# Summing the squares of the RMS norms over the d tiles with vector additions in place of partial matmuls

## The chip, the cores and the metric

The kernel runs on one core of one Trainium2 chip. The time is the device time of one execution in microseconds; where there are several runs, their median is given.

## The reference

Two layers of a trunk over 256 latent tokens and 256 context tokens of width 1024. Each layer normalises, mixes (attention and a recurrent branch), normalises again and applies a SwiGLU channel mixer, dense in layer 0 and top-2 of 8 experts in layer 1. The part that matters here is the norm, which needs the sum of squares of each token over its 1024 channels:

```python
def rms_norm(x, g):
    xf = x.astype(jnp.float32)
    y = xf * lax.rsqrt(jnp.mean(xf * xf, axis=-1, keepdims=True) + EPS)
    return (y * g.astype(jnp.float32)).astype(x.dtype)
...
    for i in range(DEPTH):
...
        a_lat = modulate(rms_norm(h_lat, mix_norm_g[i]), sh1, sc1)
        a_ctx = modulate(rms_norm(h_ctx, mix_norm_g[i]), csh1, csc1)
...
        h_lat = h_lat + g1 * o_lat
...
        h_lat = h_lat + g2 * ffn(modulate(rms_norm(h_lat, ffn_norm_g[i]), sh2, sc2))
```

## The kernel before

The residual stream is kept transposed in SBUF: `hctx` and `hlat` each hold 8 tiles (d = 0 to 7) of 128 channels by 256 tokens. Both streams together are 512 columns, one PSUM bank in f32. Because the channels lie on the partitions, a token's sum of squares goes over 8 tiles and 128 partitions.

Three passes use `stat_add` and `stat_end`. Pass 1 runs at the start, over the loaded input. Pass 2 runs inside the out-projection of layer 0 (`mixer`): when a tile d of the projection is done, `resid` adds it to the residual stream (L611), and `stat_add` squares the new tile, the context half on ScalarE and the latent half on VectorE. Pass 3 does the same in the last of the four down-projections of layer 0's FFN (`ffn`). A later norm, ahead of the experts, and the final one are computed in other functions.

In a pass, tiles 0 to 6 are each multiplied by a 128x32 block of ones (L553). The 32 output rows go to one of four strips of the bank `part`, by d mod 4, so that the bank ends with four partial sums, each 32 times over. With tile 7 ScalarE copies the bank, divided by 32 (L547), and two matmuls with a full block of ones give the sum on all partitions in the bank `ss`: one over the copy (L549), one over tile 7's squares (L550). `stat_end` then takes an inverse square root on ScalarE (`y0`, L560) and refines it with four VectorE steps (L561 to L564); `scaled` and `mod1` apply scale and shift and split the result into `ah` and `al`, with which the next matmuls begin.

Full products are made of three fp32r matmuls, L311, L312 and L313, over a high and a low half of both operands. Weights are loaded into `raw` buffers by SP's queue (L212), ScalarE makes `hi` of them (L276) and VectorE the rest, `lo` (L288); four pairs of `hi` and `lo` are held, and a new one is made when TensorE has done with an old one. An out-projection group has 24 such matmuls, a down-projection group 21.

Other work stands in between: adaLN products over weight chunks (L415 in pass 2 and after pass 3; L480 and L486 at the start, in `ada_first`), their rows' copy and transposes (L419, L422), sums over rows for `g2row` and `rbc` (L457, L459, L1103 to L1108), and warm-up matmuls at the start (L360). Which instruction stands where in an engine's queue is decided when the program is built, by a scheduler with costs of its own. The small PSUM pool "T" has two banks, and `part`, `ss` and the sums above take turns in it.

Of the kernel before, what the change touches and what calls it, by code (L numbers as in the profile page):

```python
# [12 lines left out]
AF = mybir.ActivationFunctionType  # L13
# [6 lines left out]
ND = D // P  # L20
NCTX = 256
NLAT = 256
T = NCTX + NLAT
# [165 lines left out]
class Trunk:  # L189
# [340 lines left out]
    def stat_add(self, d, t0, at):  # L530
        nc = self.nc
        n = T - t0
        if d == 0:
            self.part = self.bank("T")
        sq = self.t2k(nm="sq")
        for s in range(t0 // NCTX, 2):
            o, h = sq[:, s * NCTX - t0:(s + 1) * NCTX - t0], self.h(d, s)
            if s < SQ[at]:
                a = nc.scalar.activation(o, h, AF.Square)
            else:  # L540
                nc.vector.tensor_mul(o, h, h)
        if d == 0:
            with self.tc.issue_after(a.ins):
                self.preload(AF.Abs_reciprocal_sqrt, self.epst[0:1, 0:1])
        if d == ND - 1:
            ps = self.t2k(nm="part")
            nc.scalar.activation(ps[:, :n], self.part[:, :n], AF.Copy, scale=1.0 / 32)  # L547
            self.ss = self.bank("T")
            nc.tensor.matmul(self.ss[:, :n], lhsT=self.ones, rhs=ps[:, :n], start=True, stop=False)  # L549
            nc.tensor.matmul(self.ss[:, :n], lhsT=self.ones, rhs=sq[:, :n], start=False, stop=True)  # L550
            return
        g = 32 * (d % 4)
        nc.tensor.matmul(self.part[g:g + 32, :n], lhsT=self.ones[:, :32], rhs=sq[:, :n], start=d < 4, stop=d >= 3, tile_position=(0, g))  # L553

    def stat_end(self, t0, after=None):
        nc = self.nc
# [1047 lines left out]
```

## Time and profile before

| | |
|---|---|
| median of 3 runs | 1809.37 us (1807.25 to 1811.66) |
| profiled execution, its own time | 1812.09 us |
| its span | 1810.3 us |
| TensorE busy | 1764.0 us, 97% |
| VectorE busy | 1051.0 us, 58% |
| ScalarE busy | 824.7 us, 46% |
| HBM read | 484.94 MB, 268 GB/s over the span |
| mean granted TensorE clock | 0.984 |

Busy shares are means over stages with different limits. A row of the timeline gives an instruction's start, its duration, engine, line and operands; "x2" behind it says that neighbouring instructions were merged, and the brackets give the idle time of the engine ahead of it and what ended that. Matmuls overlap, so the distance between two starts says more than a duration. An f32 matmul appears as two instructions. PE is TensorE's matmuls, PEld its weight loads, DVE VectorE, ACT ScalarE.

### The profile page before, as it was taken

The numbers are of one execution on the slowest core, as the hardware profiler recorded it, in microseconds if no ns is written. First come the engines' busy times: TensorE is split into PE (matmuls) and PEld (weight loads), VectorE is DVE, ScalarE is ACT, GpSimd is POOL, SyncE is SP. The second block draws the span as 40 slices with busy tenths as digits, with TensorE's granted clock in tenths as the row PEclk, the third lists the DMA queues.
The fourth block names the chain that finished last, engine by engine and source line by source line (L and its number), as shares of the span: only waits on it lengthen the run. The fifth ranks groups of instructions, "written<-read, shape, count | busy, mean of one in ns | idle before, by whom it ended". The sixth has DMA issues, their size and how long they took to land. (4 is left out here: it accounts for less than half of the span.)

```text
span 1810.3 us, 22890 instructions
## 1 busy us (share of the span) xinstructions
PE 1764.0 (97%) x8645; PEld 1249.9 (69%) x8645; DVE 1051.0 (58%) x1611; ACT 824.7 (46%) x1200; POOL 0.5 (0%) x5
## 2 busy tenths in 40 slices
PE   8999999999999999999999999999999999999996
PEld 5776766888888888578887437788536883378632
DVE  4785636883555433488758119999406981189611
ACT  3674624222222222277647117777315871178512
POOL 0000000000000000000000000000000000000000
PEclk8999999999999999999999999999999999999998
DMA  9551235452534323243355999999899999999995
GB/s 383 219 206 65 68 145 199 160 199 93 181 141 182 143 89 116 94 153 113 137 221 239 388 421 421 421 421 410 343 422 421 421 420 411 421 421 420 408 416 221
DMA packets 72261, 487.55 MB, mean 269 GB/s; under 512 B 8144, under 2 KB 10576, under 8 KB 15952
## 3 DMA queue, kind: packets, MB, share of 16 engines
q1 hardware_dynamic: 71856, 485.49, 67.2%
q8 instruction: 70, 1.15, 0.2%
q10 hardware_dynamic: 288, 0.52, 0.1%
q14 instruction: 47, 0.39, 0.1%
HBM read 484.94 MB, written 1.05 MB: 268 GB/s over the span
## 5 line engine op out<-in xcount | busy, mean ns | idle before, releaser
L276 ACT ACTIVATE hi<-raw 128x1024 fp32r<-128x1024 f32 (+1 forms) x470 | 478.7, 1051 | 440.8 <-PE ps L312 316.9
L288 DVE TENSOR_TENSOR lo<-raw,hi 128x1024 fp32r<-128x1024 f32 (+1 forms) x470 | 549.1, 1211 | 105.2 <-ACT hi L276 102.9
L311 PE MATMUL ps<-ah,hi 128*128 128x512 f32 (+1 forms) x1024 | 396.6, 393 | 6.7 <-ACT ah L590 6.1
L313 PE MATMUL ps<-ah,lo 128*128 128x512 f32 (+1 forms) x1024 | 394.6, 386 | 0.0
L312 PE MATMUL ps<-al,hi 128*128 128x512 f32 (+1 forms) x1024 | 393.7, 385 | 0.0
L325 PE MATMUL ps<-hi,xe 128*128 128x512 f32 x888 | 241.4, 394 | 7.4 <-ACT hi L276 7.4
L311 PEld LDWEIGHTS ps<-ah,hi 128*128 128x128 f32 x1024 | 192.7, 189 | 61.1 <-issue 16.2
L313 PEld LDWEIGHTS ps<-ah,lo 128*128 128x128 f32 x1024 | 192.9, 188 | 45.3 <-issue 7.1
L312 PEld LDWEIGHTS ps<-al,hi 128*128 128x128 f32 x1024 | 193.4, 189 | 38.3 <-issue 2.1
L1363 PE MATMUL ps<-raw,x 128*64 128x512 f32 x896 | 202.3, 594 | 0.0
L325 PEld LDWEIGHTS ps<-hi,xe 128*128 128x128 f32 x888 | 166.8, 189 | 46.2 <-ACT hi L276 10.5
L1363 PEld LDWEIGHTS ps<-raw,x 128*64 128x64 f32 x896 | 64.5, 137 | 124.2 <-issue 123.0
L327 PE MATMUL ps<-lo,xe 128*128 128x512 f32 x444 | 139.9, 397 | 0.8 <-DVE lo L288 0.8
L1351 DVE TENSOR_TENSOR gts<-gts,ps 128x256 f32<-128x256 f32 x28 | 11.8, 422 | 211.6 <-ACT gts L1350 211.6
L1340 ACT ACTIVATE s<-ps 128x512 f32<-128x512 f32 x28 | 16.7, 597 | 221.7 <-PE ps L1363 221.7
L1386 PE MATMUL ps<-raw,gts 128*64 128x512 f32 x440 | 106.0, 599 | 0.5 <-DMA raw<-in_moe_dn_dram 0.5
L327 PEld LDWEIGHTS ps<-lo,xe 128*128 128x128 f32 x444 | 82.5, 189 | 21.3 <-issue 2.8
L611 DVE SCALAR_TENSOR_TENSOR hctx<-ps,ada,hctx 128x256 f32<-128x256 f32 x40 | 19.3, 484 | 107.8 <-PE ps L313 107.6
L325 PE MATMUL ps<-hi,ah 128*128 128x512 f32 x224 | 71.5, 400 | 0.0
L325 PE MATMUL ps<-hi,al 128*128 128x512 f32 x224 | 69.6, 392 | 0.0
L327 PE MATMUL ps<-lo,ah 128*128 128x512 f32 x224 | 69.1, 390 | 0.0
L335 ACT ACTIVATE ah<-ps 128x512 fp32r<-128x512 f32 x44 | 26.3, 599 | 92.6 <-PE ps L1258 51.5
(279 smaller groups left out, 1757.5 us busy)
## 6 DMA issues: line engine op xcount, KB each, us to landing
raw<-in_moe_up_dram SPq DMA_DIRECT2D x222, 1024.0 KB, 16.4
raw<-in_moe_dn_dram SPq DMA_DIRECT2D x111, 1024.0 KB, 17.3
raw<-in_adaw_dram SPq DMA_DIRECT2D x48, 1024.0 KB, 4.8
raw<-in_ffn_up_dram SPq DMA_DIRECT2D x28, 1024.0 KB, 4.8
raw<-in_w_in_dram SPq DMA_DIRECT2D x20, 1024.0 KB, 6.1
raw<-in_ffn_dn_dram SPq DMA_DIRECT2D x16, 896.0 KB, 4.6
raw<-in_w_out_dram SPq DMA_DIRECT2D x8, 1024.0 KB, 4.9
aux<-in_bias_dram SPq DMA_DIRECT2D x16, 192.0 KB, 3.7
```

What stands on the lines that cost most here:

```text
L276: self.his.append(self.nc.scalar.activation(hi[:, :m], raw[:, i * m:(i + 1) * m], AF.Copy))
L288: self.lastlo = self.nc.vector.tensor_sub(lo[:, :m], raw[:, i * m:(i + 1) * m], hi[:, :m])
L311: mm(out, lhsT=l[0], rhs=r[0], start=start, stop=False)
L312: mm(out, lhsT=l[0], rhs=r[1], start=False, stop=False)
L313: mm(out, lhsT=l[1], rhs=r[0], start=False, stop=stop)
L325: mm(out, lhsT=x[i], rhs=w[0][:, c], start=start and i == 0, stop=False)
L327: mm(out, lhsT=x[0], rhs=w[1][:, c], start=False, stop=stop)
L335: self.nc.scalar.activation(hi, src, AF.Copy)
L611: self.nc.vector.scalar_tensor_tensor(h, src[:, s * NCTX - t0:(s + 1) * NCTX - t0], self.ada[l][:, g, d, s:s + 1], h, ALU.mult, ALU.add)
L1340: nc.scalar.activation(s, h, AF.Copy)
L1363: nc.tensor.matmul(ps[j * SMALL:(j + 1) * SMALL], lhsT=xf[k], rhs=chs[j][:, kk * 512:(kk + 1) * 512], start=k == 0, stop=k == ND - 1, tile ...
L1386: nc.tensor.matmul(py[hf * SMALL:(hf + 1) * SMALL], lhsT=gt[f], rhs=ch[ff * 2 + hf], start=f == 0, stop=f == NF - 1, tile_position=(0, hf ...
```

## The change

The partial matmuls into strips, their bank and its copy go. The squares of tile 0 are kept, and VectorE adds the squares of tiles 1 to 6 to them, one addition per tile. With tile 7 there are two matmuls with the full block of ones, over the running sum and over tile 7's squares, into the same bank `ss`.

```diff
     def stat_add(self, d, t0, at):
         nc = self.nc
         n = T - t0
-        if d == 0:
-            self.part = self.bank("T")
         sq = self.t2k(nm="sq")
...
-        if d == ND - 1:
-            ps = self.t2k(nm="part")
-            nc.scalar.activation(ps[:, :n], self.part[:, :n], AF.Copy, scale=1.0 / 32)
+        if d == 0:
+            self.part = sq
+        elif d < ND - 1:
+            nc.vector.tensor_add(self.part[:, :n], self.part[:, :n], sq[:, :n])
+        else:
             self.ss = self.bank("T")
-            nc.tensor.matmul(self.ss[:, :n], lhsT=self.ones, rhs=ps[:, :n], start=True, stop=False)
-            nc.tensor.matmul(self.ss[:, :n], lhsT=self.ones, rhs=sq[:, :n], start=False, stop=True)
-            return
-        g = 32 * (d % 4)
-        nc.tensor.matmul(self.part[g:g + 32, :n], lhsT=self.ones[:, :32], rhs=sq[:, :n], start=d < 4, stop=d >= 3, tile_position=(0, g))
+            for i, x in enumerate((self.part, sq)):
+                nc.tensor.matmul(self.ss[:, :n], lhsT=self.ones, rhs=x[:, :n], start=i == 0, stop=i == 1)
```

The scheduler also moves instructions around the passes. Lines behind `stat_add` are three lower in the changed kernel (L608 is the old L611), the squares on VectorE have the line L539 instead of L541, and the last matmul pair has the line L550 in both.

At the start, TensorE's queue held the seven partial matmuls between the warm-up and the closing pair; the second group of adaLN matmuls stood between the first projection matmul (L311) and the second. Before:

```order
L360 MATMUL ps_86<-ones 128x128 x18
L553 MATMUL ps_115<-sq_116,ones 32x512
L553 MATMUL ps_115<-sq_122,ones 32x512
L553 MATMUL ps_115<-sq_126,ones 32x512
L553 MATMUL ps_115<-sq_130,ones 32x512
L553 MATMUL ps_115<-sq_134,ones 32x512
L553 MATMUL ps_115<-sq_138,ones 32x512
L553 MATMUL ps_115<-sq_142,ones 32x512
L549 MATMUL ps_151<-part_149,ones 128x512
L550 MATMUL ps_151<-sq_146,ones 128x512
```

The piece that follows it directly, also of before:

```order
L480 MATMUL ps_186<-raw_81,aux_71 32x256 x8
L486 MATMUL ps_197<-k,rows_195 128x2 x2
L311 MATMUL ps_182<-ah_209,hi 128x512
L480 MATMUL ps_217<-raw_165,aux_71 32x256 x8
L312 MATMUL ps_182<-al_212,hi 128x512
```

TensorE's queue at the start, after the change:

```order
L360 MATMUL ps_86<-ones 128x128 x18
L550 MATMUL ps_147<-sq_115,ones 128x512
L550 MATMUL ps_147<-sq_144,ones 128x512
L480 MATMUL ps_182<-raw_81,aux_71 32x256 x8
L486 MATMUL ps_193<-k,rows_191 128x2 x2
L480 MATMUL ps_213<-raw_161,aux_71 32x256 x8
L311 MATMUL ps_178<-ah_205,hi 128x512
L311 MATMUL ps_179<-ah_205,hi 128x512
L486 MATMUL ps_224<-k,rows_222 128x2 x2
L312 MATMUL ps_178<-al_208,hi 128x512
```

The closing pair now follows the warm-up directly, and the second L480 group stands ahead of the first L311.

At the end of pass 3, VectorE's queue from the last residual update on (`rsh` is the sum for the router's bias, `g2row` the gate row, `v` and `y` the root's steps). Before:

```order
L611 SCALAR_TENSOR_TENSOR hlat_72<-ps_5365,ada_109,hlat_72 128x256
L288 TENSOR_TENSOR lo<-raw_5598,hi 128x1024
L541 TENSOR_TENSOR sq_5389<-hlat_72 128x256
L1103 TENSOR_TENSOR rsh_5411<-small,ada_110 128x8x8
L1104 TENSOR_REDUCE rsh_5411<-rsh_5411 128x8
L1105 TENSOR_TENSOR small<-small,gs_112 128x256
L561 TENSOR_SCALAR v_5427<-ps_5394 128x512
L459 TENSOR_TENSOR g2row<-ps_5404,g2row 128x512
L562 TENSOR_TENSOR y_5426<-y_5425 128x512
L459 TENSOR_TENSOR g2row<-ps_5407,g2row 128x512
L1108 TENSOR_TENSOR rbc<-ps_5416,rbc 128x8
L563 TENSOR_TENSOR v_5427<-v_5427,y_5426 128x512
```

The same place in VectorE's queue after the change, with the two residual updates and the last addition ahead of it:

```order
L546 TENSOR_TENSOR sq_5164<-sq_5164,sq_5351 128x512
L608 SCALAR_TENSOR_TENSOR hctx_70<-ps_5355,ada_109,hctx_70 128x256
L608 SCALAR_TENSOR_TENSOR hlat_72<-ps_5355,ada_109,hlat_72 128x256
L1100 TENSOR_TENSOR rsh_5399<-small,ada_110 128x8x8
L539 TENSOR_TENSOR sq_5379<-hlat_72 128x256
L1101 TENSOR_REDUCE rsh_5399<-rsh_5399 128x8
L1102 TENSOR_TENSOR small<-small,gs_112 128x256
L459 TENSOR_TENSOR g2row<-ps_5392,g2row 128x512
L288 TENSOR_TENSOR lo<-raw_5586,hi 128x1024
L459 TENSOR_TENSOR g2row<-ps_5395,g2row 128x512
L558 TENSOR_SCALAR v_5415<-ps_5382 128x512
L1105 TENSOR_TENSOR rbc<-ps_5404,rbc 128x8
```

The last square now stands ahead of the lo split, and both g2row additions and the split stand ahead of the root's first step. On ScalarE one copy of `g2row` moves ahead of `y0`.

At the end of pass 2, TensorE's queue from the last projection matmul on, before:

```order
L313 MATMUL ps_2348<-ah_2081,lo 128x512
L415 MATMUL ps_2158<-raw_2383,aux_71 32x512 x4
L549 MATMUL ps_2380<-part_2378,ones 128x512
L550 MATMUL ps_2380<-sq_2375,ones 128x512
L422 MATMUL ps_2391<-k,rows_2389 128x128 x4
L415 MATMUL ps_2416<-raw_2414,aux_71 32x512 x4
```

The same place in TensorE's queue after the change:

```order
L313 MATMUL ps_2342<-ah_2077,lo 128x512
L550 MATMUL ps_2372<-sq_2114,ones 128x512
L415 MATMUL ps_2152<-raw_2375,aux_71 32x512 x4
L422 MATMUL ps_2383<-k,rows_2381 128x128
L550 MATMUL ps_2372<-sq_2369,ones 128x512
L422 MATMUL ps_2383<-k,rows_2381 128x128 x3
```

The first closing matmul moves ahead of the adaLN group, and one of the four transposes (L422) moves ahead of the second.

## Rows read from the trace of the kernel before

**Rows 1.** Busy time by stage: window, length, then busy us per engine, PEclk, DMA share, GB/s.

```profile
246.00:279.00 33.00, 33.00 (x136) 20.78 (x135) 10.01 (x17) 5.46 (x8) 0.00 (x0) 1.00 0.35 128
283.00:288.00 5.00, 4.20 (x37) 1.30 (x35) 4.15 (x11) 1.30 (x3) 0.00 (x0) 1.00 0.98 360
730.00:760.00 30.00, 30.00 (x118) 20.15 (x116) 11.79 (x20) 6.62 (x10) 0.00 (x0) 1.00 0.22 79
1000.00:1800.00 800.00, 784.17 (x3581) 484.21 (x3579) 445.33 (x489) 387.04 (x493) 0.00 (x0) 0.99 0.98 405
```

**Rows 2.** Timeline of TensorE around partial matmuls of pass 3.

```profile
749.65 0.39 PE L311 MATMUL ps<-ah,hi 128*128 128x512 f32 x1
...
750.33 0.39 PE L311 MATMUL ps<-ah,hi 128*128 128x512 f32 x1
...
750.78 0.39 PE L313 MATMUL ps<-ah,lo 128*128 128x512 f32 x1
...
751.12 1.02 PE L553 MATMUL ps<-sq,ones 128*32 128x512 f32 x2
...
752.41 0.39 PE L312 MATMUL ps<-al,hi 128*128 128x512 f32 x1
...
757.08 1.04 PE L553 MATMUL ps<-sq,ones 128*32 128x512 f32 x2
```

**Rows 3.** Timeline of ScalarE and VectorE in the same group.

```profile
749.29 0.40 ACT L539 ACTIVATE sq<-hctx 128x256 f32<-128x256 f32 x1
...
750.56 0.42 DVE L541 TENSOR_TENSOR sq<-hlat 128x256 f32<-128x256 f32 x1
...
754.46 0.48 DVE L611 SCALAR_TENSOR_TENSOR hctx<-ps,ada,hctx 128x256 f32<-128x256 f32 x1 [3.48 <-PE ps L313]
```

**Rows 4.** Timeline of the start, all engines.

```profile
1.06 7.23 PE L360 MATMUL ps<-ones 128*128 128x128 f32 x36 [1.06 <-DVE epst L362]
...
6.60 0.76 DVE L541 TENSOR_TENSOR sq<-hlat 128x256 f32<-128x256 f32 x2 [0.57 <-DMA hlat<-in_hT_dram]
...
8.22 3.36 PE L553 MATMUL ps<-sq,ones 128*32 128x512 f32 x14
...
12.26 1.13 PE L549 MATMUL ps<-part,ones 128*128 128x512 f32 x2 [0.69 <-ACT part L547]
...
14.28 0.69 ACT L560 ACTIVATE y<-ps,epst 128x512 f32<-128x512 f32 x1 [2.07 <-PE ps L550]
...
21.31 0.80 PE L311 MATMUL ps<-ah,hi 128*128 128x512 f32 x1 [4.95 <-ACT ah L590]
...
22.03 1.94 PE L480 MATMUL ps<-raw,aux 128*32 128x256 f32 x16
```

**Rows 5.** Busy time and granted clock of short windows at the start.

```profile
17.00:17.50 0.50, 0.00 (x0) 0.00 (x0) 0.50 (x4) 0.00 (x0) 0.00 (x0) 1.00 1.04 442
17.50:18.00 0.50, 0.00 (x0) 0.00 (x0) 0.46 (x2) 0.00 (x0) 0.00 (x0) 0.50 1.01 426
...
27.40:27.70 0.30, 0.30 (x2) 0.22 (x1) 0.30 (x1) 0.22 (x1) 0.00 (x0) 0.50 1.05 437
```

**Rows 6.** Timeline of the end of pass 2.

```profile
281.05 0.59 ACT L419 ACTIVATE rows<-ps 128x512 f32<-128x512 f32 x1
...
282.17 1.02 PE L550 MATMUL ps<-sq,ones 128*128 128x512 f32 x2
...
288.35 1.21 PE L311 MATMUL ps<-ah,hi 128*128 128x512 f32 x4 [1.16 <-ACT ah L590]
```

**Rows 7.** Timeline of VectorE at the end of pass 3.

```profile
761.34 1.22 DVE L288 TENSOR_TENSOR lo<-raw,hi 128x1024 fp32r<-128x1024 f32 x1
...
764.89 0.69 DVE L561 TENSOR_SCALAR v<-ps 128x512 f32<-128x512 f32 x1 [1.22 <-ACT y L560]
...
766.10 0.68 DVE L562 TENSOR_TENSOR y<-y 128x512 f32<-128x512 f32 x1
```

**Rows 8.** Waits of SP's queue, 1000 to 1800 us: total, times, longest.

```profile
SPq L212 <- DMA raw<-in_moe_up_dram: 159.2, 89, 2.1
```

## The prediction

> **What bounds the kernel now.** I first cut the span into stages with the busy-time view, then read the two places where the statistic stands inside matrix work row by row, then the three places where a pass ends and its statistic is waited for. In the out-projection of layer 0 and in the last down-projection of its FFN, TensorE is busy for the whole of the window (33.00 of 33.00 us and 30.00 of 30.00 us), the DMA engines are used 0.35 and 0.22, VectorE about a third [rows 1]. So there every TensorE microsecond is a microsecond of the kernel. Later, from 1000 to 1800 us, the expert weights set the pace: DMA share 0.98, 405 GB/s [rows 1].
>
> **Passes 2 and 3: the 14 partial matmuls.** An f32 matmul stands in the trace as two instructions. In an undisturbed stretch three fp32r matmuls take 750.33 - 749.65 = 0.68 us, 0.227 us each [rows 2]. Around a partial matmul the matmul before starts at 750.78 and the second one behind it at 752.41: 1.63 us, where two steps would be 0.45 us; the insertion costs 1.18 us [rows 2]. The second way: from one partial matmul to the next, 751.12 to 757.08, are 5.96 us, and 21 ordinary matmuls stand between; 21 x 0.227 = 4.76 us leave 1.20 us [rows 2]. The price holds because these matmuls come one by one, each between two full-width ones. Seven per pass go, in two passes: 14 x 1.20 = **16.8 us off**. The lower bound is the pair's own busy time, 14 x 1.02 = 14.3 us [rows 2]; I take 1.20, since both countings of whole intervals agree on it.
>
> **The additions that replace them** are six per pass, 128x512 f32; the nearest operation of that shape on VectorE, the square of y, took 0.68 us [rows 7]. In a group of the pass VectorE idles 3.48 us before the residual update [rows 3], so of 5.97 us it is busy 2.5; with the addition 3.2 us, against the 4.76 us that the group will last without its partial matmul. The addition needs ScalarE's square, which ended at 749.69, and VectorE's own, which ended at 750.98 [rows 3]; so it waits for nobody. Behind it in the queue stand the next residual update and the next lo split; the idle 3.48 us covers both. The cost is 0 as long as the addition stays under about 2 us; without that cover it would be 6 x 0.68 = 4.1 us a pass.
>
> **End of pass 2.** Before, the partial bank is copied by ScalarE, then two matmuls follow, the second waiting for the last square. The copy goes and the matmul over the sum of seven stands right behind the last projection matmul. But the last square is as late as before, and the order puts one transpose ahead of its matmul. That transpose needs a copy of rows which stood at 281.05 for 0.59 us [rows 6] and now comes some 0.4 us later, because the adaLN matmuls it reads follow the first statistic matmul. The statistic's last matmul stood at 282.17 and moves to about 282.4 in the old count; two small ada additions now stand ahead of the first VectorE step of the root. TensorE idles 1.16 us there for the modulated input [rows 6], so the delay shows: **+0.3** (bounds 0 and +0.6).
>
> **End of pass 3.** VectorE did a lo split of 1.22 us ahead of the last square, and then waited 1.22 us for y before the first step of the root [rows 7]. In the new order the square comes first, the lo split behind it, and both additions to g2row, which stood inside the root's chain and have the shape of the 0.68 us operation [rows 7], ahead of it. The wait is filled with work that was due anyway. Counting the queue through (square at 1.5 us after the last matmul's start, not 2.5; ScalarE's y behind one g2s copy; then split and additions; the root from 4.8, as before, but no longer interrupted twice) the modulated input comes **1.1 us** earlier. Bounds: 0, and the whole wait of 1.22.
>
> **Pass 1, the head.** Here TensorE has nothing else to do, so no matmul time is gained; the sum is now a chain on VectorE. From 7.36 us (two squares from 6.60, 0.76 [rows 4]) four squares at 0.38 and six additions at about 0.65 are left: 5.4 us, the sum stands at 12.8, where the first closing matmul stood at 12.26 [rows 4]. Two closing matmuls and y then take 14.28 - 12.26 = 2.02 us [rows 4], at the same clock: y 0.5 us late.
> The clock is the open point. TensorE now ends its warm-up at about 8.2 us, after 7 us of it, where the partial matmuls used to start [rows 4], and idles 4.6 us. The rows show one such gap: of 4.95 us ahead of the first projection matmul [rows 4], and in it the granted clock went from 1.00 to 0.50 (2.4 to 1.2 GHz) at about 17.5 us and still stood there just before 27.7 [rows 5]. If it falls in the new gap too, the closing pair takes up to 2.0 us more: y is 0.5 to 2.5 late. The Trainium skill, "TensorE: Matmul & The Clock Gate", Part 1, says that the slow state is the default, activity lifts it and idling brings it back; that speaks against this edit, which takes TensorE's only work out of the gap; the fall at 17.5 us, in an idle stretch, agrees with it. By that rule the head is at the late end, without it at the early one.
> Against that stands the new order. The adaLN matmuls for d = 1, which stood between the first projection matmul and the second for 1.94 us at the low clock [rows 4], now run in the wait, and the two lo splits of the first weight chunk stand ahead of xn, in gaps of the root. That gives back about 1.9 us. So: -1.4 at full clock, +0.6 at most if the clock falls; +2.5 if nothing is given back. I take the fallen clock and, since not all of the doubling lies on the path (the last instruction's drain doesn't double), **0**.
>
> **The sum.** -16.8 + 0.3 - 1.1 + 0 = **-17.6 us**. The profiled execution took 1812.1 us (span 1810.3), so it would become 1794.5; the median of the runs is 2.7 us lower, which gives **1791.8 us**, 1.0% less. Nothing between the passes and the end should absorb it: weight loads wait in SP's queue for buffers that VectorE and TensorE free, or for the load before, as 89 of them do in the expert stage for 159.2 us in all [rows 8]. A stage that is bound by loads starts earlier when its first buffers come free earlier, and then lasts as long as it did.
>
> **The rivals.**
> *The clock stays up in the head.* Same passes, head at -1.4: 1790.4 us. For it: before the gap stand 7 us of dense matmuls, where the gap in the trace followed lighter work. Against: the gap is nearly as long.
> *Pass 2's gain is lost again.* Behind pass 2 the DMA engines are at 0.98 for five microseconds [rows 1]. If those loads, and not the statistic, set the start of the FFN, its 8.4 us turn into a wait and the time is 1809.4 - 17.6 + 8.4 = 1800.2. Against: the window before is at 0.35, and the loads follow buffers which the same pass frees.
> *No difference.* The expert stage runs at 0.98 of the DMA engines; if its first loads did not move with TensorE, all of it would end where it ends now: about 1809. The only thing for it is that share.
> *Slower.* The additions hold VectorE's queue: if ScalarE's square came after VectorE's, the addition would wait, the next lo split with it, and TensorE for that split. It becomes a loss when a group takes over 5.97 us, that is when the addition with its wait costs more than 5.97 - 2.5 = 3.5 us; at 5 us it would be 14 x 1.5 = 21 us slower, 1830. The rows have ScalarE 1.3 us ahead [rows 3].
>
> **Chances and range.** Forecast 0.59, clock up 0.20, pass 2 lost 0.13, no difference 0.05, slower 0.03. What this measurement can tell from no change is about 0.2%, 3.6 us: faster 0.92, same 0.05, slower 0.03. The bounds give -14.3 + 0.6 + 0 + 2.5 = -11.2, so 1798.2, and -16.8 + 0 - 1.2 - 1.4 = -19.4, so 1790.0; the three runs lie within 2.3 us of their median, which I add below and hardly above, where all bounds would have to meet: 1787.5 to 1798.5. It holds the first two cases.
>
> **What would show it.** Right: in both passes the ordinary matmuls follow each other at 0.227 us with no gap of 1 us, and the groups of the last down-projection last 4.76 us; additions of about 0.7 us with no wait ahead of them on VectorE; the end of pass 2 as late behind its last matmul as before or a little later; the start of the expert loads some 17 us earlier. Wrong: a wait of TensorE for lo in either pass, a wait for weights at the start of the FFN, expert loads that start earlier and end no earlier, or a granted clock that stays at 1.2 GHz well past 30 us.

## The result, and the profile after

The changed kernel takes **1791.43 us** (median of 4 runs, 1786.31 to 1793.56) against 1808.31 us of the kernel before on the same chip (4 runs, 1806.21 to 1811.66): ratio 0.9898, 95% interval 0.9878 to 0.9919. Its profiled execution took 1793.56 us, with a span of 1791.8 us (1810.3 before).

The first view is the busy time by stage in the changed kernel, in the same windows moved to where the stages now are: window, length, busy us of PE, PEld, DVE, ACT and POOL, granted clock, DMA share, GB/s.

```profile
239.00:272.00 33.00, 33.00 (x152) 25.45 (x151) 16.21 (x26) 6.83 (x10) 0.00 (x0) 1.00 0.50 188
275.00:280.00 5.00, 4.80 (x38) 1.69 (x38) 3.25 (x9) 0.84 (x2) 0.00 (x0) 1.00 0.89 324
715.00:744.00 29.00, 29.00 (x129) 24.01 (x129) 18.19 (x30) 7.88 (x12) 0.00 (x0) 1.00 0.31 109
982.00:1782.00 800.00, 783.73 (x3575) 483.02 (x3573) 445.85 (x491) 387.41 (x493) 0.00 (x0) 0.99 0.98 405
```

Beside [rows 1]: TensorE is still busy without a gap in both passes and does 152 instructions in 33 us where it did 136. VectorE went from 10.01 of 33 us to 16.21, and from 11.79 of 30 to 18.19 of 29. The expert stage is as it was (DMA 0.98, 405 GB/s).

The next view is the timeline of ScalarE, VectorE and TensorE in pass 3 of the changed kernel, one group and the start of the next, and under it the group of all additions (count, shortest, median and longest ns, first and last start).

```profile
731.69 0.40 ACT L537 ACTIVATE sq<-hctx 128x256 f32<-128x256 f32 x1
...
732.96 0.42 DVE L539 TENSOR_TENSOR sq<-hlat 128x256 f32<-128x256 f32 x1
...
733.20 0.39 PE L313 MATMUL ps<-ah,lo 128*128 128x512 f32 x1
733.42 0.39 PE L311 MATMUL ps<-ah,hi 128*128 128x512 f32 x1
733.48 0.69 DVE L546 TENSOR_TENSOR sq<-sq,sq 128x512 f32<-128x512 f32 x1
733.65 0.39 PE L312 MATMUL ps<-al,hi 128*128 128x512 f32 x1
...
735.66 0.48 DVE L608 SCALAR_TENSOR_TENSOR hctx<-ps,ada,hctx 128x256 f32<-128x256 f32 x1 [1.49 <-PE ps L313]
...
740.43 0.48 DVE L608 SCALAR_TENSOR_TENSOR hctx<-ps,ada,hctx 128x256 f32<-128x256 f32 x1 [1.48 <-PE ps L313]
```

```profile
L546 DVE TENSOR_TENSOR sq<-sq,sq x18: 684/692/694, 8.6 to 743.0; 128x512 f32<-128x512 f32 x18
```

The matmuls follow each other at 0.22 to 0.23 us with nothing between. A group lasts 740.43 - 735.66 = 4.77 us. The addition takes 0.69 us, starts 0.1 us behind the square ahead of it, and leaves VectorE 1.49 us of idle where [rows 3] had 3.48.

To say where the time came from I cut each profiled execution at five marks: ScalarE's first square of pass 2, the last projection matmul of pass 2, the first matmul of the FFN, the last projection matmul of pass 3, the first matmul of the next mixer. These are the marks of the changed kernel, then those of before that [rows 6] does not show, with the block of adaLN matmuls that stood ahead of the last one.

```profile
231.64 0.40 ACT L537 ACTIVATE sq<-hctx 128x256 f32<-128x256 f32 x1
...
272.23 0.40 PE L313 MATMUL ps<-ah,lo 128*128 128x512 f32 x1
...
281.48 1.20 PE L311 MATMUL ps<-ah,hi 128*128 128x512 f32 x4 [1.19 <-ACT ah L587]
...
744.76 0.40 PE L313 MATMUL ps<-ah,lo 128*128 128x512 f32 x1
...
753.75 0.73 PE L311 MATMUL ps<-ah,hi 128*128 128x512 f32 x2
```

```profile
230.00 0.40 ACT L539 ACTIVATE sq<-hctx 128x256 f32<-128x256 f32 x1
...
279.04 0.39 PE L313 MATMUL ps<-ah,lo 128*128 128x512 f32 x1
...
760.00 0.39 PE L313 MATMUL ps<-ah,lo 128*128 128x512 f32 x1
...
767.55 3.62 PE L415 MATMUL ps<-raw,aux 128*32 128x512 f32 x26 [0.66 <-DVE g2row L459]
771.10 0.50 PE L311 MATMUL ps<-ah,hi 128*128 128x512 f32 x1
```

The lengths between the marks, in us, for these two and the twelve kernels of the experiments below; "rest" is what lies behind the last mark:

```
                       start  pass 2  its end  FFN+pass 3  its end    rest    span
before                230.00   49.04     9.31      471.65    11.10  1039.20  1810.3
after                 231.64   40.59     9.25      463.28     8.99  1038.05  1791.8
e1_head_before        229.92   40.59     9.25      463.20     8.99  1034.05  1786.0
e2_head_only          231.81   49.04     9.30      471.58    11.11  1039.06  1811.9
e3_head_warm          232.25   40.60     9.25      463.23     9.00  1034.27  1788.6
e4_double_add         229.38   40.59     9.25      463.17     8.99  1038.02  1789.4
e5_pass2_only         230.82   40.59     9.25      472.02    11.11  1037.71  1801.5
e6_pass3_only         230.87   49.04     9.31      463.21     9.00  1033.17  1794.6
e7_full_width         231.30   47.49     9.86      470.72     9.13  1037.30  1805.8
e8_packed             229.74   45.09     9.30      468.17    11.11  1035.79  1799.2
e9_after_filled       230.88   40.59     9.26      463.16     8.99  1033.92  1786.8
e10_before_filled     231.21   49.04     9.30      471.69    11.11  1035.55  1807.9
e11_old_head_filled   230.56   40.59     9.25      463.18     9.00  1034.32  1786.9
e12_head_only_filled  229.59   49.03     9.31      471.63    11.11  1034.63  1805.3
```

Between before and after: start +1.64, pass 2 -8.45, its end -0.06, FFN with pass 3 -8.37, its end -2.11, rest -1.15, together -18.5. The four lengths in the middle repeat within about 0.1 us wherever the code is the same, but for one of 0.4 us (e5). Start and rest do not: the same code takes 229.4 to 231.8 and 1033.2 to 1039.2 us. So what belongs to the change in those two had to be told apart from scatter.

### The profile page after: what moved, and what is told of

Its sections match the earlier page's. It is cut to its first block, busy times and chain, and to the rows that moved or that the text cites. A ratio compares the mean times of both kernels' runs of the same rounds, so it can differ in the third digit from the quotient of the medians.

```text
span 1791.8 us, 22827 instructions
## 1 busy us (share of the span) xinstructions
PE 1743.3 (97%) x8603; PEld 1246.2 (70%) x8603; DVE 1062.3 (59%) x1629; ACT 823.5 (46%) x1197; POOL 0.5 (0%) x5
## 3 DMA queue, kind: packets, MB, share of 16 engines
q8 instruction: 70, 1.15, 0.3%
## 5 line engine op out<-in xcount | busy, mean ns | idle before, releaser
L311 PE MATMUL ps<-ah,hi 128*128 128x512 f32 (+1 forms) x1024 | 394.8, 392 | 5.4 <-ACT ah L587 4.3
L311 PEld LDWEIGHTS ps<-ah,hi 128*128 128x128 f32 x1024 | 192.2, 189 | 55.2 <-issue 8.1
L325 PEld LDWEIGHTS ps<-hi,xe 128*128 128x128 f32 x888 | 166.7, 189 | 46.3 <-ACT hi L276 10.5
L1383 PEld LDWEIGHTS ps<-raw,gts 128*64 128x64 f32 x440 | 30.3, 136 | 53.9 <-issue 50.7
```

Source lines behind the costliest of these rows:

```text
L311: mm(out, lhsT=l[0], rhs=r[0], start=start, stop=False)
L325: mm(out, lhsT=x[i], rhs=w[0][:, c], start=start and i == 0, stop=False)
L1383: nc.tensor.matmul(py[hf * SMALL:(hf + 1) * SMALL], lhsT=gt[f], rhs=ch[ff * 2 + hf], start=f == 0, stop=f == NF - 1, tile_position=(0, hf ...
```

## The experiments

**One pass at a time.** In four kernels stat_add keeps the changed form except for the passes named, which get their partial matmuls, the copy and the closing pair back:

```diff
...
+        if at in (0,):        # e1; (1, 2) in e2, (0, 2) in e5, (0, 1) in e6
+            if d == ND - 1:
+                ps = self.t2k(nm="part")
+                nc.scalar.activation(ps[:, :n], self.strips[:, :n], AF.Copy, scale=1.0 / 32)
...
+            g = 32 * (d % 4)
+            nc.tensor.matmul(self.strips[g:g + 32, :n], lhsT=self.ones[:, :32], rhs=sq[:, :n], start=d < 4, stop=d >= 3, tile_position=(0, g))
+            return
```

e1, additions in passes 2 and 3 alone. 

> The changed kernel, but pass 1 (the head) keeps its partial matmuls; passes 2 and 3 use additions. Theory (the head loses, the passes win): the fourth adaLN group (L480, d = 3) stood at 34.09 us before and at 35.54 after; here it is back near 34.1, and the time is about 1.5 us under the changed kernel, near 1790.0, ratio to the kernel before 0.989. Rival (the head's loss in that one profile was only its loads, which landed later): the group stands near 35.5 again or the time is that of the changed kernel, 1791.4.

Measured: 1789.82 us (6 runs, 1787.19 to 1793.05), ratio 0.9897 (0.9877 to 0.9916), against the changed kernel's 0.9898. The whole gain is in passes 2 and 3. The 1.5 us that the expectation gave the head do not hold: the fourth adaLN group (L480, d = 3) stood at 33.54 us here, but in all profiles with the old head it stands at 33.54 to 34.74 and in those with additions at 33.35 to 35.54 (e3 left out), so 34.09 against 35.54 was one pair out of a scatter.

e2, additions in pass 1 alone. 

> Additions in pass 1 alone; passes 2 and 3 keep their partial matmuls. Theory: 1.5 us slower than the kernel before (1808.3), 1809.8, too little to tell from the time alone; in the trace the L480 group of d = 3 stands 1.5 us later than the 34.09 us of before, at about 35.5, and the last projection matmul of pass 2 at about 280.5. Rival (pass 1 gains as well as the others): 1805, with that group at 33 us.

Measured: 1813.12 us (10 runs, 1810.16 to 1814.38) against 1808.73 of before, measured beside it: ratio 1.0019, 1.0006 to 1.0032. By these numbers the head costs 3 to 4 us (3.4 by the ratio, 4.4 by the medians). Its profile doesn't have them in the head: the start is 231.81 us, 0.6 above the longest with the old head (229.92 to 231.21), and the rest is as long as before's, 1039.06. This contradiction is what the last four kernels were made for.

e5, pass 2 alone. 

> Additions in pass 2 alone, partial matmuls in passes 1 and 3. Theory: 7 x 1.20 = 8.4 us off, nothing lost behind it: 1799.9, and the first projection matmul of the FFN 8.3 us before its 288.35. Rival (the FFN start waits for loads): the last projection matmul comes 8.3 us earlier but the FFN's first does not, time near 1808.

Measured: 1803.52 us (10 runs), ratio 0.9955 (0.9938 to 0.9971); three runs lie at 1797.5 to 1798.1 and seven at 1803.0 to 1804.7. In the table pass 2 has its 8.45 us off and pass 3 nothing.

e6, pass 3 alone. 

> Additions in pass 3 alone, partial matmuls in passes 1 and 2. Theory: 8.4 us off for the seven matmuls and 1 to 2 us for the new order behind the pass: 1798.3. If the order is worth nothing: 1799.9.

Measured: 1802.74 us (10 runs), ratio 0.9961 (0.9946 to 0.9975); two runs at 1796.4 and 1797.4, eight at 1801.5 to 1803.5. In the table pass 3 and its end have 10.5 us off, pass 2 nothing. The lengths of the passes add up; the medians of these two kernels can't be used to half a per cent, since each falls into two bunches some 6 us apart.

**Does the clock matter in the head?** e3 is the changed kernel, with the old partial matmuls of pass 1 as well, into a bank that nobody reads:

```diff
...
+        if at == 0 and d < ND - 1:
+            g = 32 * (d % 4)
+            nc.tensor.matmul(self.strips[g:g + 32, :n], lhsT=self.ones[:, :32], rhs=sq[:, :n], start=d < 4, stop=d >= 3, tile_position=(0, g))
```

> The changed kernel with the old partial matmuls of pass 1 issued as well, into a bank that nobody reads; passes 2 and 3 as in the changed kernel. It tells the two causes of the late head apart. If the low clock is the larger part: the granted clock stays at 1.00 through the closing pair, the pair takes 2.0 us to y and not 3.8, and y comes 1.8 us earlier, near 15.9 us for a sum that is ready at 13.9. If the chain of additions is all of it: the pair takes as long as in the changed kernel and y stays near 17.7.

Measured: one run, 1790.42 us. This is its closing pair:

```profile
14.55 1.98 PE L555 MATMUL ps<-sq,ones 128*128 128x512 f32 x4 [1.23 <-DVE sq L551]
```

The granted clock stayed at 1.00 until 20 us and the closing pair took 1.98 us, where the changed kernel's took 3.78 at 0.50; y came at 16.57 us. But the start is 232.25 us, the longest of all. Its squares came late in that execution (an addition waited 1.44 us for ScalarE's square), so the length alone is no proof that the clock is worth nothing; it gives no sign that it is worth something.

**What covers the additions.** e4 repeats each addition of passes 2 and 3 into a spare tile:

```diff
             nc.vector.tensor_add(self.part[:, :n], self.part[:, :n], sq[:, :n])
+            if at:
+                nc.vector.tensor_add(self.t2k(nm="spare")[:, :n], self.part[:, :n], sq[:, :n])
```

> The changed kernel with a second addition of the same shape behind each of the six in passes 2 and 3, into a buffer that nobody reads: 12 more VectorE operations of 0.69 us. Theory (VectorE idles 1.5 us or more in each group, so additions are covered): the time of the changed kernel, 1791.4, within 0.5 us. Rival (each addition is on the path): 12 x 0.69 = 8.3 us more, 1799.7.

Measured: 1791.85 us (4 runs, 1791.22 to 1791.90), ratio 0.9905 (0.9882 to 0.9928); pass 2 takes 40.59 us and FFN with pass 3 463.17, as with one addition. The timeline of VectorE in e4 shows what paid:

```profile
735.89 0.69 DVE L546 TENSOR_TENSOR sq<-sq,sq 128x512 f32<-128x512 f32 x1
736.62 0.69 DVE L548 TENSOR_TENSOR spare<-sq,sq 128x512 f32<-128x512 f32 x1
738.06 0.48 DVE L610 SCALAR_TENSOR_TENSOR hctx<-ps,ada,hctx 128x256 f32<-128x256 f32 x1 [0.75 <-PE ps L313]
```

The wait ahead of the residual update is 0.75 us instead of 1.49; the second addition came out of it. So by estimate an addition is free here up to about 2.2 us (0.69 + 1.49); no run tried more than the two of 0.69.

**What the 1.20 us are.** e7 leaves the additions out of passes 2 and 3 and sums all eight squares on TensorE, with the full 128 columns of ones, straight into the closing bank (no strips, no copy):

```diff
+        if at:
+            if d == 0:
+                self.ss = self.bank("T")
+            nc.tensor.matmul(self.ss[:, :n], lhsT=self.ones, rhs=sq[:, :n], start=d == 0, stop=d == ND - 1)
+            return
```

> Pass 1 as changed; in passes 2 and 3 no additions and no strips: each tile's squares are multiplied by the full 128x128 ones into the bank of the sum, 8 matmuls a pass where the changed kernel has 2. It prices the matmul apart from the 32-column strip. If the strip's switch is part of the 1.20 us: a full-width insertion costs about 0.9 us, 12 of them 10.8 us, time 1802.2. If 1.20 us is the price of any f32 matmul between fp32r ones: 12 x 1.20 = 14.4 us, 1805.8.

Measured: 1807.08 us (10 runs, in two bunches at 1801 and 1807.5), ratio 0.9977 (0.9960 to 0.9994). Pass 2 is 47.49 - 40.59 = 6.90 us longer than with additions, 0.99 us for each of the seven that stand inside it; FFN with pass 3 is 470.72 - 463.28 = 7.44 us longer, 1.06 each. The expectation counted six per pass; there are seven, 14 in all, and their price lies between its two cases of 0.9 and 1.20. A full-width matmul cost a little less than one on a 32-column strip (8.45 / 7 = 1.21).

e8 keeps the strips, but holds them back, and issues those of d = 0 to 3 behind the fourth square and those of d = 4 to 6 behind the seventh:

```diff
+        if at:
+            self.held = [] if d == 0 else self.held
+            self.held.append(sq)
...
+            if d in (3, 6):
+                for k in range(4 * (d // 4), d + 1):
+                    g = 32 * (k % 4)
+                    nc.tensor.matmul(self.strips[g:g + 32, :n], lhsT=self.ones[:, :32], rhs=self.held[k][:, :n], start=k < 4, stop=k >= 3, tile_position=(0, g))
...
```

> Pass 1 as changed; in passes 2 and 3 the partial matmuls are held back until tile 3 and tile 6 are squared and then issued together; as built, each pass has runs of 3, 1, 2 and 1 of them, in different strips. If strips side by side run at once (the four of an adaLN group, 8 instructions, take about 1.2 us together): four insertions of about 1.2 us a pass and the copied bank, 2 x 4.8 = 9.6 us over the changed kernel, 1801.0. If each matmul costs its 1.20 us wherever it stands: 14 x 1.20 = 16.8 us, 1808.2.

Measured: 1802.89 us (10 runs, in two bunches at 1800 and 1806), ratio 0.9961 (0.9944 to 0.9977). In the queue they came as runs of 3, 1, 2 and 1 in each pass (in pass 2 the run of three stood inside an adaLN group). This is TensorE in pass 3 of e8, around the run of three and the run of one:

```profile
728.40 0.39 PE L313 MATMUL ps<-ah,lo 128*128 128x512 f32 x1
728.72 1.06 PE L551 MATMUL ps<-sq,ones 128*32 128x512 f32 x6
...
730.05 0.39 PE L312 MATMUL ps<-al,hi 128*128 128x512 f32 x1
...
731.20 0.40 PE L311 MATMUL ps<-ah,hi 128*128 128x512 f32 x1
731.53 1.04 PE L551 MATMUL ps<-sq,ones 128*32 128x512 f32 x2
...
732.84 0.39 PE L313 MATMUL ps<-ah,lo 128*128 128x512 f32 x1
```

From the matmul before to the second behind it: 730.05 - 728.40 = 1.65 us for three, 732.84 - 731.20 = 1.64 for one. Three partial matmuls on three strips cost what one does, 1.65 - 2 x 0.227 = 1.20 us. So the price is one per run of strips, not one per matmul. The Trainium skill, "TensorEngine Tiling (Array Packing)", Key Properties, says that different tiles of the array can work in parallel; the run of three agrees with it. Four runs per pass at 1.20 would be 4.8 us; the passes are 4.50 and 4.89 us longer than with additions.

But the price is not the interruption alone. Behind pass 2 of the changed kernel 16 adaLN matmuls of the same shape follow each other on the four strips, with nothing between them:

```profile
276.65 3.64 PE L415 MATMUL ps<-raw,aux 128*32 128x512 f32 x32
```

That is four groups of four in 3.64 us, 0.91 us a group. So about 0.9 of the 1.20 us is what a run on strips takes among its own kind, and by estimate about 0.3 us comes of standing between fp32r matmuls of full width. No run took these two apart, and none issued the partial sums as fp32r, which might have cost much less.

**The two bunches.** In ten profiles the granted clock fell to 0.50 in the router stage, at about 925 to 945 us, in six (before, after, e2, e4, e5, e7: 10.2 to 13.7 us low) and not in four (e1, e3, e6, e8). The rest was 1037.3 to 1039.2 us in the six and 1033.2 to 1035.8 in the four. First TensorE in the changed kernel and its windows, then e1, the end of its wait and a window behind it:

```profile
922.91 0.96 PE L956 MATMUL ps<-ur 128*128 128x256 f32 x6
924.94 0.27 PE L1011 MATMUL ps<-mskr,ur 128*128 128x8 f32 x1 [1.07 <-DVE mskr L1008]
...
929.64 0.63 PE L1201 MATMUL ps<-oh,Xl 128*128 128x128 f32 x2
```

```profile
924.00:926.00 2.00, 1.06 (x9) 1.06 (x10) 1.90 (x13) 1.98 (x5) 0.00 (x0) 1.00 0.79 332
926.00:928.00 2.00, 2.00 (x18) 2.00 (x16) 2.00 (x6) 1.45 (x4) 0.00 (x0) 0.82 0.00 0
928.00:930.00 2.00, 2.00 (x11) 2.00 (x11) 2.00 (x14) 1.18 (x3) 0.00 (x0) 0.50 0.03 8
```

```profile
923.07 0.27 PE L1024 MATMUL ps<-mskr,ur 128*128 128x8 f32 x1 [1.07 <-DVE mskr L1021]
```

```profile
926.00:928.00 2.00, 2.00 (x21) 2.00 (x20) 2.00 (x13) 1.08 (x3) 0.00 (x0) 1.00 0.00 0
```

The fall stands behind a wait of 1.07 us for the router's mask, which all ten profiles have. The record also gives the mean granted clock of every run, and it separates the bunches: in e5 to e8 the 14 shorter runs have 0.986 to 0.989, the 26 longer ones 0.983 to 0.985 (a mean lower by 0.003 to 0.004 is, by estimate, 11 to 14 us at half clock, as long as the fall). The same holds for e2: six of its ten runs have 0.982 or 0.983, of the 17 of before beside it only two, and at 0.983 its five took 1812.8 to 1814.0 us, the two of before 1814.0 and 1814.4. A line of idle-time matmuls (L956) stands there already. The last four kernels lengthen it, in four versions of the norms: the changed one (e9), before (e10), e1's (e11) and e2's (e12):

```diff
-HEAT = (6, 6, 8)
+HEAT = (6, 15, 8)
```

> The changed kernel with one number changed outside the passes: behind the router's two logit matmuls TensorE runs 15 idle-time matmuls instead of 6, so that its wait of 1.07 us for the expert mask is filled. In the ten profiles so far the granted clock falls to 0.50 right behind this wait in six (10.2 to 13.6 us low) and not in the other four, and the stage behind the last norm takes 1037.3 to 1039.2 us in those six and 1033.2 to 1035.8 us in the four. Theory: that fall, and not the norms, makes equal runs of one kernel differ by 6 us, and it goes with the idle TensorE ahead of it; filled, no fall at the router, stage 1033 to 1035 us, runs within about 3 us of each other around 1787. Rival: the fall does not hang on this wait; the runs spread as before, 1786 to 1794, median 1790 to 1791.5.

Measured: 1788.20 us (5 runs, 1784.80 to 1789.61), ratio to before 0.9875 (0.9852 to 0.9898).

> The kernel before with the same 15 idle-time matmuls. Theory: without the fall at the router its runs lie at the fast end of what the kernel before showed, 1805.5 to 1808, and the difference to the changed kernel with the same filler is the sum of the stages of the passes, 16.5 to 18.5 us, with little scatter. Rival: 1805.5 to 1814.5 as before, median 1808.5 to 1809.5.

Measured: 1807.44 us (12 runs, 1805.49 to 1809.77), ratio 0.9984 (0.9972 to 0.9997); the kernel before, measured beside it, 1809.57 (23 runs, 1805.39 to 1813.97).

> Pass 1 with its partial matmuls, passes 2 and 3 with additions, and the 15 idle-time matmuls. Theory that the additions in the head cost nothing that can be told: within 1 us of the changed kernel with the filler, about 1787. Rival that they cost what the head-only kernel's median showed (1813.12 against 1808.7): 3 us or more faster than the changed kernel with the filler.

Measured: 1787.02 us (5 runs, 1784.65 to 1788.63), ratio 0.9869 (0.9847 to 0.9892).

> Additions in pass 1 alone, and the 15 idle-time matmuls. Theory that the head-only kernel's 3 to 4 us more were runs in which the clock fell at the router, not the head: within 1 us of the kernel before with the filler, 1805.5 to 1808. Rival that the head costs 3 to 4 us by itself: 1809 to 1812, beside a kernel before with the filler at 1805.5 to 1808.

Measured: 1807.43 us (12 runs, 1805.89 to 1810.15), ratio 0.9991 (0.9979 to 1.0004).

TensorE in e9 at the place of the wait, and its clock there:

```profile
922.07 2.03 PE L956 MATMUL ps<-ur 128*128 128x256 f32 x15
924.10 0.27 PE L1011 MATMUL ps<-mskr,ur 128*128 128x8 f32 x1
```

```profile
926.00:928.00 2.00, 2.00 (x20) 2.00 (x20) 2.00 (x7) 1.67 (x6) 0.00 (x0) 1.00 0.03 8
```

None of the four profiles has the fall, and the rest is 1033.9 to 1035.6 us in all of them. All 34 runs of the four kernels have a mean clock of 0.986 to 0.989, while eight of the 23 of before beside them have 0.983 or 0.984. The kernel before loses its longest runs: the longest is 1809.8 us instead of 1814.0. So a large part of the scatter was the clock at the router, and that hangs on the idle TensorE ahead of it. With the scatter smaller the head can be read: before and head-only are equal (1807.44 and 1807.43), and the changed kernel and the one with the old head overlap (1788.2 and 1787.0, a difference of 1.2 us in runs that spread over 4 to 5). The 3 to 4 us of e2 were not in the head. All four are below their unfilled versions' medians, though only for before was the unfilled kernel measured beside it; e9 and e11 have the lowest medians of all kernels here.

## Why the prediction was right, and where it was not

The forecast was 1791.8 us and the median 1791.43. The mechanism held; the closeness is partly luck: both ends of the passes came out shorter than forecast, so that the stages gave 19.0 us and not 17.6, and the scatter of the medians, in which the clock at the router takes part, hid it.

**Passes 2 and 3, -16.8.** Right: -8.45 and -8.37, 1.20 us for each partial matmul. The step "from one partial matmul to the next" was the right measure, the pair's own busy time (14.3) too little. That it is paid once per run of strips, e8 shows, so "because these matmuls come one by one" stands; but about 0.9 of the 1.20 us is what such matmuls take among their own kind, and only the rest comes of the full-width neighbours.

**The additions, 0.** Right: 0.692 us, at most 0.1 us of idle time ahead of any of the 18, and e4 shows that twice as many are still covered. The limit of about 2 us that the prediction gave is not contradicted; e4 tried 1.4.

**End of pass 2, +0.3.** Mis-sized: -0.06. The transposes' copy did come later (2.32 us behind the last projection matmul instead of 2.01), as said. Two steps were wrong: the copy was to move the last statistic matmul from 282.17 to about 282.4, and two small additions that "now stand ahead of the first VectorE step of the root" were to delay that step. Here is the changed kernel's end of pass 2:

```profile
274.55 0.60 ACT L419 ACTIVATE rows<-ps 128x512 f32<-128x512 f32 x1 [0.70 <-PE ps L415]
...
275.37 1.02 PE L550 MATMUL ps<-sq,ones 128*128 128x512 f32 x2
...
276.43 0.69 ACT L557 ACTIVATE y<-ps,epst 128x512 f32<-128x512 f32 x1 [1.28 <-PE ps L550]
...
277.15 0.69 DVE L558 TENSOR_SCALAR v<-ps 128x512 f32<-128x512 f32 x1
```

The last statistic matmul starts 275.37 - 272.23 = 3.14 us behind the projection, before 3.13 [rows 6]; the first step of the root 4.92 us, before 4.91. The copy came 0.31 us later and not 0.4, and with the one transpose behind it held the last statistic matmul no longer than the first one had before. The small additions ran while VectorE waited for ScalarE's y, which ended at 276.43 + 0.69 = 277.12, 0.03 us ahead of the root's first step, so they cost nothing there; and the root, with two of them fewer inside it, is 0.07 us shorter (2.85 us from its first step to xn, before 2.92).

**End of pass 3, -1.1.** Mis-sized: -2.11, beyond its bound of -1.22. The step that failed is that the modulated input alone sets the start. VectorE's chain came out a little better than counted. Here is its first xn, before and after:

```profile
768.93 0.48 DVE L573 SCALAR_TENSOR_TENSOR xn<-hctx,gs,v 128x256 f32<-128x256 f32 x1
```

```profile
752.27 0.48 DVE L570 SCALAR_TENSOR_TENSOR xn<-hctx,gs,v 128x256 f32<-128x256 f32 x1
```

That is 8.93 and 7.51 us behind the last projection matmul, 1.42 us sooner where 1.1 were counted. But before, TensorE was not waiting for it: at 767.55 it began a block of adaLN matmuls (26 instructions in 3.62 us), which a g2row addition had held up, and the mixer's first matmul stood behind them until 771.10. In the changed kernel:

```profile
748.82 0.69 DVE L459 TENSOR_TENSOR g2row<-ps,g2row 128x512 f32<-128x512 f32 x1
...
750.16 3.62 PE L415 MATMUL ps<-raw,aux 128*32 128x512 f32 x26 [0.21 <-DVE v L558]
```

With both g2row additions ahead of the root, the block waits for the root's first step alone, and begins 5.40 us behind the last projection matmul instead of 7.55; the whole 2.1 us go through to the mixer. e7, whose order has both g2row additions ahead of the root too, ends the pass in 9.13 us; e8, which has them inside the root as before, in 11.11. No run moved these additions alone, so that they are the cause is read from the timelines.

**Pass 1, 0.** Right in the sum, over 13 profiles: with the old head the start is 229.92 to 231.21 us (six, mean 230.56), with additions 229.38 to 231.81 (seven, mean 230.62; e3 left out). The +1.64 between the two profiles is scatter. The parts went as the late end of the count said:

```profile
13.12 0.68 DVE L546 TENSOR_TENSOR sq<-sq,sq 128x512 f32<-128x512 f32 x1
...
13.86 3.78 PE L550 MATMUL ps<-sq,ones 128*128 128x512 f32 x4 [6.33 <-DVE sq L546]
...
17.68 0.69 ACT L557 ACTIVATE y<-ps,epst 128x512 f32<-128x512 f32 x1 [7.10 <-PE ps L550]
```

```profile
10.00:12.00 2.00, 0.00 (x0) 0.00 (x0) 2.00 (x6) 0.58 (x2) 0.00 (x0) 1.00 1.02 418
12.00:14.00 2.00, 0.14 (x1) 0.14 (x1) 1.89 (x5) 0.00 (x0) 0.00 (x0) 0.62 1.02 428
14.00:16.00 2.00, 2.00 (x3) 0.97 (x4) 0.00 (x0) 0.00 (x0) 0.00 (x0) 0.50 1.04 438
```

TensorE idled 6.33 us, the clock fell to 1.2 GHz in the gap, as in [rows 5], and the closing pair took 3.78 us. y came at 17.68, where it stood at 14.28 [rows 4]; in the other six such heads it came at 15.97 to 16.57, in the six old heads at 13.73 to 14.38. The pair starts at 13.86 here and at 12.27 to 12.75 in the other six, where the prediction had 12.8. By the Trainium skill's rule in "TensorE: Matmul & The Clock Gate", Part 1, that the prediction weighed, the fall was due; the trace agrees. In the mean over these seven heads and six old ones y came 2.4 us later with additions (16.53 for 14.08) and the first projection matmul 2.5 (23.60 for 21.11), but the fourth adaLN group (L480, d = 3) only 0.2 (34.42 for 34.24). So what was lost is given back between those two. That the adaLN matmuls in the wait and the earlier lo splits gave it back is the count of the prediction; no run took it apart. The rival "clock stays up in the head" fell with the windows above.

**The other rivals.** Pass 2's gain was not lost at the FFN (its end 9.25 us against 9.31), the expert stage moved with TensorE (rest no longer than before), and no addition held VectorE's queue. The price of the slower rival was counted with 14 additions; there are 12, so it would be 18 us and not 21.

**The sum.** The four lengths in the middle give -8.45 - 0.06 - 8.37 - 2.11 = -19.0 us, where the prediction had -17.6. The two filled kernels, e9 and e10, differ by 1807.44 - 1788.20 = 19.2. The median of the four runs differed by 16.9; the 2 us between are within the scatter of medians of four runs, of which the clock at the router is a part.

## What to carry to other kernels

Price a small matmul that stands inside a stream of full ones by the distance that it opens between its neighbours, compare that with what the same matmul takes among its own kind, and look whether the engine next door idles in each group for as long as the replacement takes. Where a stream ends, ask which engine really starts the next one: here it was a block of matmuls that waited for an addition nobody would have put on the critical path. When runs of one kernel fall into bunches, cut the traces at marks and compare stage by stage before believing a difference of medians, even one whose interval excludes no change.

## What the runs showed that I had not expected

Equal code differed by 6 us between executions: the granted clock fell at the router in six of ten profiles, behind a wait of 1.07 us that all ten have. The Trainium skill, "TensorE: Matmul & The Clock Gate", Part 1, says that the monitor behind the clock runs freely and doesn't start with the kernel, so that the point of a change varies from run to run; that the same wait is followed by a fall in some executions and not in others agrees with it. What else decides it in a given run stays open. Nine matmuls more in the wait removed the fall in four profiles of four and took about 2 us from the median of the kernel before; the fall was gone with the old norms and with the new ones.
